# Second products of gathered expert rows moved to TensorE, with a tied order, float32 one-hots and nine row buffers

## Chip, core and metric

The kernel runs on one core of one Trainium2 chip. The metric is device time in microseconds (us) of one execution, the median of three runs. Engines: TensorE (PE, its weight loads are PEld), VectorE (DVE), ScalarE (ACT), GpSimd (POOL) and SyncE (SP); the last two issue the transfers here, GpSimd the gathers and SyncE the rest.

## What is computed

Two layers over 512 tokens of 1024 features. Each layer is a token mixer (four heads of differential attention, eight of stick-breaking attention) with a norm, and then a retrieval layer ("PEER") with a norm. The change is about the second:

```
def peer_ffn(h, w_query, sub_keys, expert_u, expert_v):
    q = (xt @ w_query).reshape(T, PEER_HEADS, 2, HALF_Q)
    scores = einsum('thpc,hpnc->thpn', q, sub_keys)
    top_s, top_i = top_k(scores, 16)              # per half of a key
    cand_s = top_s[:, :, 0, :, None] + top_s[:, :, 1, None, :]
    best_s, best_pos = top_k(cand_s, 16)          # 16 of 16384 experts per head
    gate = softmax(best_s)
    act = gelu(einsum('cd,ced->ce', xc, expert_u[ic]))      # 8 heads x 16 = 128 experts a token
    return einsum('ce,ced->cd', gc * act, expert_v[ic])
```

An expert is one row of `expert_u` and one of `expert_v`, 4 KB each. All is float32.

## The kernel before

The tokens are four blocks of 128. For blocks 0 and 1 (`BLK_A`) the experts' rows are **gathered**: for each of the 128 choices an indirect DMA on GpSimd brings one row per token, 128 rows of 4 KB (line 624, tile `row`, pool `gat` with five buffers). With rows of u, VectorE multiplies by h and sums along the row (line 634, "first products": one column of `c`); then gelu and the gate; with rows of v it adds row times coefficient to `y` (line 645, "second products"). Blocks 2 and 3 (`BLK_B`) go through products with **all** experts, called dense: 32 chunks of 512 experts. `first` (line 760) makes gelu(h . u) for both blocks, `weigh` (line 791) transposes it (line 800) and multiplies it by a dense matrix of gates, `second` (line 810) multiplies by v (lines 821 to 824). Weights and factors are split into two exact parts on ScalarE (748, 806) and VectorE (750, 807), so three products stand for one. The first seven chunks make their first products in plain float32 (line 776), before the gates are known.

`select` (line 541) finds the 16 best experts of four heads on VectorE (max, max_index, match_replace, one-hots of positions). `gates` (line 657) turns a block's choices into the dense matrix: for each token a one-hot of the expert's low digit (line 700, bfloat16, four tokens at once) and three weighted one-hots of the high digit (line 711), whose products on TensorE (line 723, three for each token) go through `st` to DRAM.

The order is the kernel's own. Pieces of work are generators ("threads") that tell before each step which engines it will hold and for how long; `run_threads` (line 110) takes the step that can start first, and gives its instructions a priority. A scheduler behind it then orders each engine's instructions by priority and its own estimate of time. Threads: `early` (the mixer of block 0), `indices` and `gathers` for blocks 0 and 1 of each layer (the four gathers take turns), and `rest` (the mixer of blocks 1, 2, 3, in which `gates` is started for blocks 2 and 3, then `dense`). The mixer's projections are lines 438 and 444, its output projection line 481, the queries line 507, the scores line 513. Buffers come from pools: `t4` (18 of 4 KB per partition), `d2` (18 of 2 KB), `st` (4), `ps` (8 in PSUM).

## Time and profile before

| | us |
|---|---|
| runs: median (lowest to highest) | 3537.8 (3537.52 to 3541.9) |
| profiled execution, span | 3535.5 |
| TensorE busy | 2765.6 (78%) |
| VectorE busy | 2937.8 (83%) |
| ScalarE busy | 1184.8 (34%) |
| GpSimd busy | 1681.0 (48%) |
| DMA moved | 1032.89 MB, mean 292 GB/s |

One execution was profiled; its span is the time from the first to the last instruction. Busy times are unions of an engine's instructions. Read the stages by what they hold: 163 to 827 us is the gathering of block 0 in layer 0, 878 to 1753 that of block 1, 1898 to 2571 and 2623 to 3508 the same in layer 1; the dense products run from 1108 to 1820 and from 2857 to 3513.

### The profile page before, as it was taken

What the parts mean: (1) busy time and instruction counts of PE and PEld (TensorE: products, weight loads), DVE (VectorE), ACT (ScalarE), POOL (GpSimd) and SP (SyncE); (2) the same over time, 40 slices, a digit from 0 to 9 for tenths busy, and PEclk for the clock granted to TensorE, in tenths of its full rate; (3) what the DMA queues carried; (4) which work ended last, traced back from release to release, by engine and by line L of the source; (5) the groups of instructions that cost most, each with busy time, mean ns of one, the idle gap of its engine ahead of it and who ended that gap; (6) DMA issues with size and microseconds to landing.
All of it is one profiled execution on the core that took longest, in us unless ns stands there. A gap on an engine that the chain in (4) does not pass through costs nothing.

```text
span 3535.5 us, 42200 instructions
## 1 busy us (share of the span) xinstructions
PE 2765.6 (78%) x14604; PEld 2214.2 (63%) x14604; DVE 2937.8 (83%) x5537; ACT 1184.8 (34%) x1900; POOL 1681.0 (48%) x1297
## 2 busy tenths in 40 slices
PE   7996474468576999999997876834694679999997
PEld 5776462366245888888776764613652468888885
DVE  2577889989998888888668678999799987888888
ACT  2114640411133444444231138404110434444442
POOL 0265645763675433334314655457536743344443
PEclk9997587579777999999998886865796689999998
DMA  5698796686769999999966987955966799999996
GB/s 228 212 329 294 246 333 201 206 302 231 261 222 360 360 347 343 349 351 348 369 222 253 331 286 237 351 177 196 337 220 232 256 367 343 349 346 354 345 344 251
DMA packets 283926, 1032.89 MB, mean 292 GB/s; under 512 B 25152, under 2 KB 91200, under 8 KB 231488
## 3 DMA queue, kind: packets, MB, share of 16 engines
q0 software_dynamic: 147456, 536.94, 42.4%
q1 hardware_dynamic: 136256, 493.26, 37.6%
q8 instruction: 115, 1.88, 0.2%
q14 instruction: 99, 0.81, 0.1%
HBM read 991.30 MB, written 38.80 MB: 291 GB/s over the span
## 4 chain that ended last, share of the span: by engine, by line
PE 40%; DVE 14%; issue 6%; DMA 5%; POOL 2%; ACT 2%; POOLq 0%; DVEq 0%; ACTq 0%
PE ps L822 7%; PE ps L821 7%; PE ps L824 6%; PE ps L786 5%; PE ps L785 5%; PE ps L784 5%; DVE row L634 3%; DMA row<-u,idx 2%; DVE ha L645 2%; POOL row L624 2%; DMA row<-v,idx 2%; PE ps L800 1%; DVE d L711 1%; DVE idf L586 1%; DVE d L579 1%
## 5 line engine op out<-in xcount | busy, mean ns | idle before, releaser
L624 POOL DMA_INDIRECT row<-v,idx x512 | 669.3, 1307 | 892.6 <-DVE ha L645 662.5
L624 POOL DMA_INDIRECT row<-u,idx x512 | 655.2, 1280 | 589.1 <-DVE row L634 375.9
L634 DVE SCALAR_TENSOR_TENSOR row<-row,ha 128x1024 f32<-128x1024 f32 x512 | 666.6, 1315 | 121.0 <-DMA row<-u,idx 118.1
L645 DVE SCALAR_TENSOR_TENSOR ha<-row,c,ha 128x1024 f32<-128x1024 f32 x508 | 700.3, 1379 | 58.0 <-DMA row<-v,idx 53.9
L750 DVE TENSOR_TENSOR t<-st,t 128x1024 fp32r<-128x1024 f32 x449 | 533.2, 1224 | 210.8 <-ACT t L748 210.7
L748 ACT ACTIVATE t<-st 128x1024 fp32r<-128x1024 f32 x456 | 453.9, 1056 | 36.6 <-PE ps L824 15.8
L723 PE MATMUL ps<-d,d 128*128 128x128 bf16 x1536 | 218.4, 295 | 207.0 <-DVE d L711 128.8
L821 PE MATMUL ps<-t,d 128*128 128x512 f32 x1024 | 314.2, 398 | 44.5 <-ACT d L806 44.5
L822 PE MATMUL ps<-t,d 128*128 128x512 f32 x1024 | 342.3, 395 | 0.0
L723 PEld LDWEIGHTS <-d 128*128 128x128 bf16 x1536 | 178.6, 121 | 234.5 <-issue 192.5
L824 PE MATMUL ps<-t,d 128*128 128x512 f32 x1024 | 316.7, 390 | 0.0
L785 PE MATMUL ps<-t,t 128*128 128x512 f32 x800 | 311.5, 389 | 0.5 <-DVE t L750 0.5
L786 PE MATMUL ps<-t,t 128*128 128x512 f32 x800 | 311.7, 390 | 0.0
L784 PE MATMUL ps<-t,t 128*128 128x512 f32 x800 | 304.2, 389 | 1.0 <-ACT t L748 1.0
L507 PE MATMUL ps<-t,st 128*128 128x128 f32 x2048 | 263.2, 293 | 35.2 <-DMA st<-w_query 35.2
L507 PEld LDWEIGHTS ps<-t,st 128*128 128x128 f32 x2048 | 257.8, 209 | 41.5 <-issue 29.5
L444 PE MATMUL ps<-t,st 128*128 128x128 f32 x2048 | 243.0, 281 | 22.2 <-ACT t L191 16.2
L444 PEld LDWEIGHTS ps<-t,st 128*128 128x128 f32 x2048 | 238.9, 197 | 28.6 <-ACT t L191 18.6
L821 PEld LDWEIGHTS ps<-t,d 128*128 128x128 f32 x1024 | 190.4, 190 | 82.4 <-ACT d L806 45.5
L822 PEld LDWEIGHTS ps<-t,d 128*128 128x128 f32 x1024 | 190.1, 190 | 47.0 <-DVE t L750 10.2
L824 PEld LDWEIGHTS ps<-t,d 128*128 128x128 f32 x1024 | 192.2, 188 | 40.9 <-DVE d L807 0.3
L806 ACT ACTIVATE d<-t 128x512 fp32r<-128x512 f32 x128 | 78.7, 632 | 410.9 <-DVE t L803 410.9
(175 smaller groups left out, 4190.8 us busy)
## 6 DMA issues: line engine op xcount, KB each, us to landing
st<-ut SPq DMA_DIRECT2D x128, 1024.0 KB
st<-vd SPq DMA_DIRECT2D x128, 1024.0 KB
st<-w_in SPq DMA_DIRECT2D x48, 1024.0 KB
st<-w_query SPq DMA_DIRECT2D x48, 1024.0 KB
gd<-st SPq DMA_DIRECT2D x32, 1024.0 KB
t<-gd SPq DMA_DIRECT2D x64, 512.0 KB
st<-w_o SPq DMA_DIRECT2D x24, 1024.0 KB
ln<-ln SPq DMA_DIRECT2D x16, 512.0 KB
```

What stands on the lines that cost most here:

```text
L444: nc.tensor.matmul(ps[:, f * P:(f + 1) * P], lhsT=w(c, slice(f * P, (f + 1) * P)), rhs=hT[:, c, :], start=(c == 0), stop=(c == DC - 1))
L507: nc.tensor.matmul(ps[:, f * P:(f + 1) * P], lhsT=w(c, slice(f * P, (f + 1) * P)), rhs=hq[b][0][:, c, :], start=(c == 0), stop=(c == DC - 1))
L624: nc.gpsimd.indirect_dma_start(out=g, out_offset=None, in_=src, in_offset=bass.IndirectOffsetOnAxis(ap=idx[s // (NSEL // 2)][:, s % (NSEL ...
L634: nc.vector.scalar_tensor_tensor(g, g, 1.0, h1, op0=ALU.mult, op1=ALU.mult, accum_out=c[:, s:s + 1])
L645: nc.vector.scalar_tensor_tensor(y, g, c[:, s:s + 1], y, op0=ALU.mult, op1=ALU.add)
L750: (nc.gpsimd if eng == "POOL" else nc.vector).tensor_tensor(lo, part, hi.bitcast(F32), op=ALU.subtract)
L784: nc.tensor.matmul(ap[b], lhsT=xhi, rhs=hi[:, c, :], start=(d == 0), stop=False)
L785: nc.tensor.matmul(ap[b], lhsT=xhi, rhs=lo[:, c, :], start=False, stop=False)
L786: nc.tensor.matmul(ap[b], lhsT=xlo, rhs=hi[:, c, :], start=False, stop=(d == DC - 1))
L821: nc.tensor.matmul(y[b][n], lhsT=shi, rhs=hi[:, n, :], start=start, stop=False)
L822: nc.tensor.matmul(y[b][n], lhsT=shi, rhs=lo[:, n, :], start=False, stop=False)
L824: nc.tensor.matmul(y[b][n], lhsT=slo, rhs=hi[:, n, :], start=False, stop=stop)
```

## The change

1. **Second products on TensorE** (`token_products`). The choices are transposed (`idxT`), so that an indirect DMA brings the 128 v rows of one token, one per partition. The coefficients are transposed too, and laid into two windows `win` of 32 x 32 columns that hold zeros but for every 32nd column. A matmul with 32 columns of a window as weights adds one token's sum to one row of a 32-row group of PSUM. A step takes two tokens and two halves of 512 columns, four matmuls in four groups of 32 rows (`quarter`), which are kept next to each other. So 64 steps replace the 128 additions of a block.
2. **Tied order** (`Traced`, `bound`). The instructions that a step emits on an engine are made to follow those of steps that were planned at least 8 us earlier on that engine, so the scheduler cannot move them far from the plan. Dots and token steps are planned six gathers behind their gather (`AWAY`), and `cost` has a resource that a step may wait for without being held up in the plan (`soft`).
3. **Gates from float32 one-hots**: two VectorE instructions for each token (one with two scalars: equal, times the gate), one float32 product instead of three in bfloat16, none on GpSimd or ScalarE.
4. **Buffers**: nine rows in flight instead of five, 12 `d2` instead of 18, 17 `t4` instead of 18.
5. `gates` gets more weight among the threads (lead 40 instead of 6), and `early` of layer 1 starts only when the gates of layer 0 are planned.

```diff
-    t4p = ctx.enter_context(tc.tile_pool(name="t4p", bufs=18))
+    t4p = ctx.enter_context(tc.tile_pool(name="t4p", bufs=17))
-    gat = ctx.enter_context(tc.tile_pool(name="gat", bufs=5))
-    d2p = ctx.enter_context(tc.tile_pool(name="d2p", bufs=18))
+    gat = ctx.enter_context(tc.tile_pool(name="gat", bufs=9))
+    d2p = ctx.enter_context(tc.tile_pool(name="d2p", bufs=12))
...
+    def bound(start):
+        for n, log in nc.log.items():
+            m = marks[n]
+            while len(m) > 1 and m[1][0] <= start - REACH:
+                m.pop(0)
+            if log and m and m[0][0] <= start - REACH:
+                for ins in log:
+                    tc.add_manual_dep(ins, m[0][1], nosync, reason="plan")
+            if log:
+                m.append((start, log[-1].name))
+                log.clear()
...
-                        spawn(gates(l, b), 6.0)
+                        spawn(gates(l, b), 40.0)
...
+    def token_products(src, idxT, c, y):
+        yield cost(lat=2.0, PE=0.3, ACT=0.4)
+        ct = psum()
+        nc.tensor.transpose(ct[:, :P], c, ident)
+        cT = a2()[:, :P]
+        nc.scalar.copy(cT, ct[:, :P])
+        H = 32
+        for s in range(2):
+            for q in range(2):
+                nc.scalar.copy(wins[q].rearrange("p (i z) -> p i z", z=H)[:, :, H - 1],
+                               cT[:, (2 * s + q) * H:(2 * s + q + 1) * H])
+            ps = psum()
+            todo = []
+            def products(i, rows):
+                at = (H - 1) * i + H - 1
+                def quarter(q, a):
+                    o = H * (2 * a + q)
+                    return nc.tensor.matmul(ps[o:o + H, :], lhsT=wins[q][:, at:at + H],
+                                            rhs=rows[q][:, a * 512:(a + 1) * 512],
+                                            start=(i == 0), stop=(i == H - 1))
+                first = quarter(1, 0)
+                with tc.high_priority(offset=90000), tc.issue_after(first.ins):
+                    for q, a in ((1, 1), (0, 0), (0, 1)):
+                        quarter(q, a)
+            for i in range(H):
+                yield cost(lat=2.1, soft="PE", PE=0.95, POOL=2.08, DMA=3.2)
+                if len(todo) == AWAY // 2:
+                    products(*todo.pop(0))
+                rows = []
+                for q in range(2):
+                    g = gat.tile([P, D], F32, name="row")
+                    t = (2 * s + q) * H + i
+                    nc.gpsimd.indirect_dma_start(out=g, out_offset=None, in_=src,
+                                                 in_offset=bass.IndirectOffsetOnAxis(ap=idxT[:, t:t + 1], axis=0))
+                    rows.append(g)
+                todo.append((i, rows))
...
+            o = a2()
+            nc.scalar.copy(o, ps)
+            for a in range(2):
+                nc.sync.dma_start(y[64 * s:64 * s + 64, a * 512:(a + 1) * 512], o[64 * a:64 * a + 64, :])
...
-            yield pace(1.14)
-            g = row(ur[l], s)
-            nc.vector.scalar_tensor_tensor(g, g, 1.0, h1, op0=ALU.mult, op1=ALU.mult, accum_out=c[:, s:s + 1])
+            yield pace(1.3)
+            if len(todo) == AWAY:
+                dot(*todo.pop(0))
+            todo.append((s, row(ur[l], s)))
...
+        if b in TOK:
+            yield from token_products(vr[l], picks[l, b][2], c, y)
...
+        def hots(t):
+            hot, w = (fold(a2(), NT) for _ in range(2))
+            for k in range(NT):
+                nc.vector.tensor_scalar(hot[:, k, :], iota_b, ijg[:, 1, t + k:t + k + 1], None, op0=ALU.is_equal)
+                nc.vector.tensor_scalar(w[:, k, :], iota_b, ijg[:, 0, t + k:t + k + 1],
+                                        ijg[:, 2, t + k:t + k + 1], op0=ALU.is_equal, op1=ALU.mult)
+            return hot, w
...
             for n in range(NT):
-                for k, w in enumerate(ws):
-                    nc.tensor.matmul(ps[:, n * P:(n + 1) * P], lhsT=hot[:, 1, :, n], rhs=w[:, :, n],
-                                     start=(k == 0), stop=(k == 2))
+                nc.tensor.matmul(ps[:, n * P:(n + 1) * P], lhsT=hot[:, n, :], rhs=w[:, n, :],
+                                 start=True, stop=True)
...
     def early(l, b):
+        if l > 0:
+            yield f"gates {l - 1} {BLK_B[-1]}"
         yield from mixer(l, [b], [(b, None)], [[b]])
```

How the order moves is seen at two places. In the built program of the change most instructions carry the line of the wrapper, L70, and are told apart by their tiles.

VectorE, gates of block 3 in layer 0, before. Lines 700 and 711 are the one-hots, line 634 the first products of block 1:

```order
1024 L700 TENSOR_TENSOR d_5240<-iota_b,d_5180 128x512 x2
1025 L634 SCALAR_TENSOR_TENSOR row,c<-row,ha 128x1024 x2
1026 L711 TENSOR_TENSOR d_5243<-d_5240,d_5181 128x512
1027 L700 TENSOR_TENSOR d_5263<-iota_b,d_5180 128x512 x2
1028 L634 SCALAR_TENSOR_TENSOR row,c<-row,ha 128x1024 x2
1029 L711 TENSOR_TENSOR d_5266<-d_5263,d_5181 128x512
```

and the end of the same gates in the change (`iota_b` marks a one-hot, `row,c<-row,ha` a first product, `ha<-ha` the residual of block 0):

```order
1243 L70 TENSOR_SCALAR d_6078<-iota_b,d_5512 128x128
1244 L70 TENSOR_SCALAR d_6079<-iota_b,d_5512 128x128
1245 L70 SCALAR_TENSOR_TENSOR ha<-ha 128x1024
1246 L70 SCALAR_TENSOR_TENSOR row,c<-row,ha 128x1024 x2
1247 L70 BN_STATS aln_st<-ha 128x6 x2
```

The first products stood between the one-hots; now they stand behind the last of them, and block 0's residual and norm with them.

TensorE, second half of dense in layer 0, before. Line 784 to 786 are first products, 822 and 824 second products:

```order
3396 L822 MATMUL ps<-t_9451,d_9207 128x512 x2
3397 L824 MATMUL ps<-t_9450,d_9208 128x512 x2
3398 L785 MATMUL ps<-t_9474,t_3051 128x512
3399 L786 MATMUL ps<-t_9473,t_3050 128x512
3400 L784 MATMUL ps<-t_9473,t_3051 128x512
```

and in the change (`row,win` is a token step, two quarters in a line):

```order
2733 L70 MATMUL ps<-t_12215,d_11981 128x512 x2
2734 L70 MATMUL ps<-t_12214,d_11982 128x512 x2
2735 L70 MATMUL ps<-row,win_115 32x512 x2
2736 L70 MATMUL ps<-row,win_114 32x512 x2
2737 L70 MATMUL ps<-t_12240,d_11971 128x512 x2
2738 L70 MATMUL ps<-t_12240,d_11981 128x512 x2
```

The token steps of block 1 stand singly among dense's matmuls, each behind its two gathers; the additions that they replace stood on VectorE among the parts of the weights.

## Rows read from the trace of the kernel before

**Rows 1.** The page: busy us of each engine, and the two large DMA queues.

```profile
PE 2765.6 (78%) x14604; PEld 2214.2 (63%) x14604; DVE 2937.8 (83%) x5537; ACT 1184.8 (34%) x1900; POOL 1681.0 (48%) x1297
...
q0 software_dynamic: 147456, 536.94, 42.4%
q1 hardware_dynamic: 136256, 493.26, 37.6%
```

**Rows 2.** Busy time by stretch: from:to, length, engines' busy us, clock, DMA share, GB/s.

```profile
147.00:440.00 293.00, 220.15 (x1432) 184.73 (x1431) 238.15 (x583) 108.86 (x215) 170.99 (x136) 0.81 0.80 279
440.00:1087.00 647.00, 397.05 (x2163) 291.63 (x2161) 608.33 (x1362) 165.17 (x321) 376.05 (x311) 0.75 0.71 252
1087.00:1820.00 733.00, 706.72 (x3334) 581.86 (x3333) 587.73 (x673) 310.00 (x399) 280.60 (x194) 0.98 0.93 346
...
2202.00:2835.00 633.00, 393.58 (x2172) 288.73 (x2171) 591.57 (x1350) 164.49 (x324) 368.32 (x301) 0.75 0.71 251
2835.00:3513.00 678.00, 653.51 (x2979) 539.20 (x2977) 563.03 (x602) 287.49 (x346) 279.47 (x186) 0.98 0.93 348
```

**Rows 3.** Groups by line on VectorE, 440 to 1087 us: busy, mean ns, idle before.

```profile
L645 DVE SCALAR_TENSOR_TENSOR ha<-row,c,ha 128x1024 f32<-128x1024 f32 x127 | 186.7, 1470 | 25.9 <-DMA row<-v,idx 24.7 <-DVE ha L645 0.2 <-issue 0.2
L634 DVE SCALAR_TENSOR_TENSOR row<-row,ha 128x1024 f32<-128x1024 f32 x73 | 106.3, 1473 | 6.0 <-DMA row<-u,idx 6.0
L700 DVE TENSOR_TENSOR d<-iota_b,d 128x512 bf16<-128x512 bf16 x122 | 67.0, 586 | 0.0
L711 DVE TENSOR_TENSOR d<-d,d 128x512 bf16<-128x512 bf16 x98 | 63.2, 673 | 0.1
```

**Rows 4.** The same view, shapes apart, whole run: a 128x128 VectorE instruction with one scalar.

```profile
L296 DVE TENSOR_SCALAR dg<-ident,rc 128x128 f32<-128x128 f32 x64 | 17.5, 293 | 0.0
```

**Rows 5.** The same view, VectorE in dense, 1110 to 1690 us (25.5 chunks).

```profile
L750 DVE TENSOR_TENSOR t<-st,t 128x1024 fp32r<-128x1024 f32 x200 | 236.3, 1220 | 90.2 <-ACT t L748 90.2
...
L634 DVE SCALAR_TENSOR_TENSOR row<-row,ha 128x1024 f32<-128x1024 f32 x52 | 64.6, 1260 | 1.4 <-DMA row<-u,idx 1.4
L807 DVE TENSOR_TENSOR d<-t,d 128x512 fp32r<-128x512 f32 x55 | 36.4, 699 | 0.4
...
L634 DVE DVE_READ_ACCUMULATOR row<-row,ha 128x1 f32 x52 | 4.2, 81 | 0.0
```

**Rows 6.** Timeline of TensorE (start us, us, instruction): two chunks' transposes that follow each other.

```profile
1383.07 1.04 PE L800 MATMUL ps<-ident,t 128*128 128x128 f32 x8
...
1405.81 1.03 PE L800 MATMUL ps<-ident,t 128*128 128x128 f32 x8
```

**Rows 7.** Timeline of TensorE: runs of equal matmuls, and the second layer's first projections.

```profile
906.58 13.04 PE L776 MATMUL ps<-st,t 128*128 128x512 f32 x30
...
1824.07 14.00 PE L481 MATMUL ps<-st,t 128*128 128x512 f32 x32 [0.81 <-ACT t L412]
...
1856.57 7.31 PE L507 MATMUL ps<-t,st 128*128 128x128 f32 x64
...
1909.45 15.75 PE L444 MATMUL ps<-t,st 128*128 128x128 f32 x119 [15.94 <-ACT t L191]
```

**Rows 8.** Timeline of TensorE: 64-column matmuls of line 373, in two column groups and in one.

```profile
1820.56 0.61 PE L824 MATMUL ps<-t,d 128*128 128x512 f32 x2
1821.10 1.58 PE L373 MATMUL ps<-d,t 128*64 128x128 f32 x16
1822.61 0.66 PE L411 MATMUL ps<-ident,t 128*128 128x128 f32 x4
...
2193.25 1.09 PE L373 MATMUL ps<-d,t 128*64 128x128 f32 x8 [0.27 <-ACT t L315]
```

**Rows 9.** Timeline of all engines: gathers on GpSimd beside line 296 on VectorE.

```profile
2188.81 0.95 POOL L624 DMA_INDIRECT row<-v,idx  x1 [1.35 <-DVE ha L645]
...
2189.33 0.47 DVE L296 TENSOR_SCALAR dg<-ident,rc 128x128 f32<-128x128 f32 x1
...
2191.07 0.95 POOL L624 DMA_INDIRECT row<-v,idx  x1 [1.31 <-DVE d L351]
```

More of the change, by code (lines that the diff above doesn't have):

```diff
@@ L47, with __init__, __getattr__, call @@
 AHEAD = 7
+TOK = [0, 1]
+REACH = 8
+AWAY = 6
 NT = 4
 NTG = len(BLK_B) * P // GT
+class Traced:
+    def __init__(self, eng, log):
+        self.eng, self.log = eng, log
+    def __getattr__(self, name):
+        f = getattr(self.eng, name)
+        if not callable(f):
+            return f
+        def call(*args, **kwargs):
+            r = f(*args, **kwargs)
+            ins = getattr(r, "ins", None)
+            if ins is not None:
+                self.log.append(ins)
+            return r
+        return call
+class TracedCore:
+    def __init__(self, nc):
+        self.log = {}
+        for n in ("tensor", "vector", "scalar", "gpsimd"):
+            self.log[n] = []
+            setattr(self, n, Traced(getattr(nc, n), self.log[n]))
+        self.sync = nc.sync
 @with_exitstack
@@ L107, in spawn @@
     def spawn(gen, lead):
-        threads.append({"gen": gen, "lead": lead, "ready": clock[0], "next": None})
+        threads.append({"gen": gen, "lead": lead, "ready": clock[0], "at": clock[0], "next": None})
+    marks = {n: [] for n in nc.log}
+    nosync = mybir.DependencyInfo(mybir.DependencyClass.NoSync, mybir.DependencyReason.DATA)
+    def bound(start):
[9 more added lines that the diff above has]
+                log.clear()
     def run_threads():
@@ L126, in run_threads @@
                     continue
-                start = max([th["ready"]] + [free[e] - slack[e] for e in th["next"][1]])
+                lat, engines, soft = th["next"]
+                start = max([th["ready"]] + [free[e] - slack[e] for e in engines if e != soft])
                 ready.append((start, th))
@@ L130, in run_threads @@
             start, th = min((x for x in ready if x[0] <= first), key=lambda x: x[1]["ready"] - x[1]["lead"])
-            lat, engines = th["next"]
+            lat, engines, soft = th["next"]
+            th["at"] = start
             for e, c in engines.items():
@@ L619, in pace @@
         def pace(dve):
-            return cost(lat=2.2, DVE=dve, POOL=1.04, DMA=1.46)
+            return cost(lat=1.2, soft="DVE" if b == BLK_A[0] else "", DVE=dve, POOL=1.04, DMA=1.6)
         def row(src, s):
@@ L638, in gathers, with add @@
         y = hap.tile([P, D], F32, name="ha")
-        for s in range(NSEL):
-            yield pace(1.2)
-            g = row(vr[l], s)
-            if s == 0:
-                nc.vector.tensor_scalar_mul(y, g, c[:, s:s + 1])
-            else:
-                nc.vector.scalar_tensor_tensor(y, g, c[:, s:s + 1], y, op0=ALU.mult, op1=ALU.add)
+        if b in TOK:
+            yield from token_products(vr[l], picks[l, b][2], c, y)
+        else:
+            def add(s, g):
+                if s == 0:
+                    nc.vector.tensor_scalar_mul(y, g, c[:, s:s + 1])
+                else:
+                    nc.vector.scalar_tensor_tensor(y, g, c[:, s:s + 1], y, op0=ALU.mult, op1=ALU.add)
+            todo = []
+            for s in range(NSEL):
+                yield pace(1.35)
+                if len(todo) == AWAY:
+                    add(*todo.pop(0))
+                todo.append((s, row(vr[l], s)))
+            for x in todo:
+                yield cost(lat=1.8, DVE=1.35)
+                add(*x)
         b2 = (l, b + 1) if b + 1 in BLK_A else (l + 1, BLK_A[0])
@@ L715, in gates, with products @@
         stg = {}
-        def products(tg, t0, hot, ws):
+        def products(tg, t0, hot, w):
             if t0 == 0:
```

79 lines of the change are left out of this document (33 added, 46 removed).

## The prediction, made before the changed kernel ran

> **What bounds the kernel now.** I read four views in this order. The page's sums show three resources that are all nearly full over the whole span: VectorE 83%, TensorE 78%, the DMA queues 42.4% + 37.6% = 80% [rows 1]. Such an average hides stages, so the table of busy time by stretch comes next [rows 2]. It shows two kinds of stretch that alternate, once per layer. From 440 to 1087 us (and 2202 to 2835) VectorE is busy 608.3 of 647 us (591.6 of 633) while TensorE is busy 397 and runs at a mean granted clock of 0.75, and DMA moves 252 GB/s: **VectorE sets the pace.** It does three jobs at once there: the second products of block 0 (line 645), the choice of experts with the one-hots of the gates, and from 880 us the first products of block 1 (line 634). From 1087 to 1820 (2835 to 3513) TensorE is busy 706.7 of 733 us at a clock of 0.98 and DMA has a share of 0.93: **TensorE sets the pace and DMA is next**, with the products of all experts ("dense"). Third, the groups of VectorE in the first kind of stretch [rows 3] give what can leave it. Fourth, the rows of single instructions give prices [rows 4 to 9].
>
> The profiled execution spans 3535.5 us; the median of the runs is 3537.8, so 2.3 us lie around the span. I make the sum on the span and add 2.3.
>
> **The change, part by part.**
>
> *Second products leave VectorE.* In 440 to 1087 the 127 additions of line 645 are 186.7 us busy, with 25.9 us of idle time before them [rows 3]; 1.47 us each. The 512 of the whole run are on no path any more in the first kind of stretch.
>
> *First products of block 1 go behind the gates.* The order shows 9 of them before the last one-hot of block 3 (none in the second layer); in the trace 73 stood there, 106.3 us and 73 reads of the accumulator at 81 ns, 5.9 us [rows 3, 5]. They are not saved: they run in the dense stretch.
>
> *One-hots in float32.* Out go lines 700 and 711 on VectorE, 67.0 + 63.2 = 130.2 us for two blocks [rows 3]. In come 256 instructions of 128x128 per block; the nearest is line 296, 17.5 us for 64, 0.273 each [rows 4], so 2 x 256 x 0.273 = 139.8. Cost 9.6 us on VectorE. GpSimd and ScalarE lose their parts of lines 700 and 711, and TensorE does 4 products for each 4 tokens instead of 12; none of them was the limit, so I price that at nothing.
>
> VectorE's work in 440 to 1087 becomes 608.3 - 186.7 - 106.3 - 5.9 + 9.6 = 319 us. How long does the stretch take then? If VectorE stayed as full as now (0.94) 319/0.94 = 339; in 147 to 440, where attention and not VectorE sets the pace, it is busy 238 of 293, 0.81 [rows 2], which gives 393. I take 0.81, since the same attention and norm waits come to light. On top comes the query projection of blocks 3 and 1, when VectorE has little to do: 512 matmuls at 7.31/64 = 0.114, 58 us, 32 of the output projection, 14 us, and about 10 us of norm and transposes: 82 us [rows 7]. The gates of block 2 now share their time with 14 token steps on TensorE (28 gathers). Beside a gather, line 296 took 0.47 us instead of 0.27, and the gather its usual 0.95 [rows 9], so 28 x 0.2 = 6 us. Together 481 instead of 647: **166 us less, in each layer.** Ends: 647 - 427 = 220 (at 0.94) and 27 (at a share of 0.60, the one of TensorE there [rows 2]).
>
> The Trainium skill, SBUF — State Buffer, section Who interferes with whom, says that a VectorE tensor_scalar in its two-port mode and GpSimd hold one port pair exclusively, and that the loser blocks fully. The rows show 0.2 us, not a gather's 0.95; by the rule the 28 gathers (18 in the second layer) would add 26 and 17 us, not 6 and 4, and the sum would be 3390.
>
> *Token steps.* A step multiplies two tokens' rows, four matmuls of 32 columns by 512 on four column groups. No such step is in the trace. A 128x512 float32 matmul takes 14.0/32 = 0.4375 us [rows 7]; four in series are 1.75, four at once 0.44. The nearest row is line 373, whose heads of odd number write the other column group: 16 of them took 1.58 us, where 8 in one group took 1.09 [rows 8], so 16 in series would take 1.09 + 8 x 0.11 = 1.97. Two groups do run at once. A visit costs something too: the second of the two of line 824 started at 1820.79, the next could have at 1821.02, and line 373 started at 1821.10; line 411 came 0.09 late likewise [rows 8]. With 0.2 for a visit and a little for the second pair's start, I take **0.68 us a step** (0.44 to 1.95). 64 steps a block are 44 us.
>
> *Dense, first layer.* A full chunk is 104 matmuls, 22.74 us [rows 6]. In the order 12 chunks hold about five token steps each, ten gathers. Their TensorE time is 22.74 + 5 x 0.68 = 26.1. Their DMA time: a gathered row set costs 0.424 x 3535.5/1024 = 1.464 us, weights 0.376 x 3535.5/493.3 = 2.695 us per MB [rows 1]; a chunk loads 4.72 MB, so 10 x 1.464 + 12.7 = 27.4 us. DMA limits there, 1.3 us a chunk. Chunks with first products hold seven rows: 10.2 + 12.7 = 23.0 us of DMA; on VectorE 8 x 1.18 + 4 x 0.66 + 7 x 1.32 = 21.3 us [rows 5], which just fits.
>
> After the gates TensorE has: 25 full chunks, 569; seven chunks with their first half done early, 22.74 x 56/104 = 12.2 each, 86; block 0 of the next layer, which before ran at the end of dense and after it and now stands at its start, 512 x 0.114 + 64 x 0.4375 + some 20 of attention, 106; 62 of the early first products, at 13.04/30 = 0.435, 27; token steps 44; DMA's excess 15; idle time as now 733 - 706.7 = 26 [rows 2, 6, 7]. Sum 873, and 30 us for the norm, the trip of h through DRAM and the transposes. So from the end of the gates to the projections of the next layer 903 us. Before it was 1087 to 1909.4, 822 [rows 7]. **Cost 80 us.** Block 0's work is paid inside dense instead of after it, and nearly all of block 1's gathers must fit in as well.
>
> *Second layer.* The first stretch again gives 166. Dense takes 678 [rows 2] and has no early block to hold: 12 chunks go from 22.74 to 27.4, +56; 13 steps at the end, +9; first products +3: **cost 68.** Tail: the result passes through a copy and a DMA, +3.
>
> *Nine row buffers.* They let a gather be issued before the buffer of five earlier is read. Where VectorE held the buffers that is a gain already counted; where DMA is full it adds nothing. The price is one t4 and six d2 buffers less; in the order a weight half still finds its place two to five halves ahead in dense, three to six before, and a half takes 2.7 us on TensorE, so nothing.
>
> Sum: -166 + 80 - 166 + 68 + 3 = -181; 3535.5 - 181 = 3354.5, and with 2.3 around it **3357 us.**
>
> **The rivals.**
>
> *Slower: the four quarters run in series.* A step then costs 1.75 + 0.2 = 1.95 us, in TensorE's own order, before every product that stands behind it. A chunk with five steps takes 22.74 + 9.75 = 32.5 instead of 27.4, 24 times: +122. The 13 steps at the end add 17, and the 64 steps in each first stretch 81, of which half lies beside idle TensorE (busy 397 of 647): +80. Total 3357 + 219 = 3576, slower than now. It decides from about 1.75 us a step on. Against it stands line 373 [rows 8]; for it, that no row has four groups.
>
> *Slower: waits take VectorE's place.* Each engine must now keep to the plan's order, so a late gather on TensorE holds the gates' products behind it, and these hold the one-hots. With VectorE at 0.60 in the first stretches they shorten by 27 us each: 3357 + 278 = 3635. It decides where each shortens by less than 76, a share of 0.66. Against it: the order has gathers six ahead of their step, and these stretches use DMA at 0.71 [rows 2].
>
> *Faster still.* VectorE stays as full as now: 220 a layer, 3357 - 108 = 3249. For it: much of that work, the choice and the gates, depends on VectorE alone.
>
> *The port lock.* If one-hots and gathers exclude each other as 28 x 0.95 and 18 x 0.95 us in the gates of block 2, the sum is 3390. The skill's sentence above is this case; the rows speak for the smaller price.
>
> *The change doesn't do what it says.* With DMA at 0.93 in dense, nine buffers may bring no more bytes there; that is the forecast already.
>
> **How the numbers follow.** Forecast 0.62, at 3357, with its own range 3280 to 3460 (steps two by two, 1.08 us, would be 3357 + 50). Faster still 0.16. Port lock 0.07. Series 0.08, waits 0.07. The range is 3225 to 3480: the two slow rivals lie above it, 0.15, and some of the fastest below. A measurement can tell about 0.2%, 7 us: faster 0.85, the same 0.02, slower 0.13.
>
> **What would show it.** In the table by stretch: the gates of block 3 end near 920 us instead of 1087, and VectorE's share in that stretch is near 0.8. The quarters of one step start within 0.1 us of each other and a step takes 0.6 to 0.8 us. In dense, chunks with first products take 23 us, those with token steps 27 to 28, with a DMA share close to 1. The projections of the second layer start near 1820 instead of 1909. The prediction is wrong if steps start one after the other, if TensorE waits for gathers in the first stretch, or if its clock falls to 1.2 GHz in dense.

## The result

| | before | change |
|---|---|---|
| median of the runs (lowest to highest), first chip | 3537.7 (3535.7 to 3541.9) | 3558.7 (3552.6 to 3565.4) |
| the same on another chip | 3543.7 (3536.4 to 3552.7) | 3536.8 (3530.6 to 3543.6) |
| profiled execution, span | 3535.5 | 3563.6 |

The ratio is 1.0061, 95% interval 1.0043 to 1.0079, on the first chip, and 0.9979 (0.9969 to 0.999) on the other, where the same program ran again. So the change is worth nothing within about half a per cent, and its sign depends on the chip. The forecast was 3357. All experiments ran beside the kernel before, whose median was 3542 to 3546 on their chips; they are compared with 3537, the change on the other chip of the table. On the three chips where the change was timed it took 3559, 3537 and 3534 us (one run); on the chips of experiments 4 and 9 and of the last two of experiment 8 it was not timed. So a difference of less than some 25 us from the change says little here.

The page of the change. Against [rows 1], VectorE lost 699 us of work and TensorE gained 264. Nearly all instructions carry the wrapper's line, L70; `row,win` is the token steps:

```profile
span 3563.6 us, 44443 instructions
...
PE 3029.1 (85%) x16148; PEld 2191.2 (61%) x16148; DVE 2238.5 (63%) x5540; ACT 1148.2 (32%) x1785; POOL 1463.9 (41%) x1170
...
q0 software_dynamic: 147456, 536.94, 41.3%
q1 hardware_dynamic: 137536, 495.36, 36.8%
...
L70 PE MATMUL ps<-row,win 128*32 128x512 f32 x2048 | 281.3, 636 | 48.6 <-DMA row<-v,idxT 48.6
```

Busy time by stretch, columns as in [rows 2]. The stretches are cut at the end of block 3's gates (907.2, 2682.5), at the end of dense in layer 0 (1906), at the next projections (1964.5) and at the end of dense in layer 1 (3549):

```profile
440.00:907.20 467.20, 385.49 (x2342) 248.52 (x2340) 335.41 (x1392) 147.68 (x268) 181.06 (x168) 0.91 0.72 264
907.20:1906.00 998.80, 918.23 (x4346) 668.01 (x4344) 568.64 (x913) 340.53 (x438) 398.88 (x280) 0.97 0.83 307
1906.00:1964.50 58.50, 4.61 (x32) 4.16 (x25) 50.55 (x80) 3.00 (x6) 44.85 (x38) 0.53 0.96 361
...
2682.50:3549.00 866.50, 803.81 (x3636) 577.98 (x3635) 508.04 (x623) 293.83 (x359) 370.34 (x269) 0.97 0.88 324
```

The stages, in us; the forecast is the prediction's own sum:

| stage | before | forecast | change | difference |
|---|---|---|---|---|
| start to the end of the gates, layer 0 | 1087 | 921 | 907 | -180 |
| to layer 1's first projections (dense) | 822 | 903 | 1057 | +235 |
| to the end of the gates, layer 1 | 926 | 760 | 718 | -208 |
| to the end (dense and tail) | 700 | 771 | 881 | +181 |

The gain in front of the gates came, and a little more of it than forecast. **Both dense stages gave all of it back.** There the miss is 154 + 110 us.

### The profile page after: what moved, and what is told of

The parts are those of the page before. It is cut to its first block, busy times and chain, and to the rows that moved or that the text cites. A ratio compares the mean times of both kernels' runs of the same rounds, so it can differ in the third digit from the quotient of the medians.

```text
span 3563.6 us, 44443 instructions
## 1 busy us (share of the span) xinstructions
PE 3029.1 (85%) x16148; PEld 2191.2 (61%) x16148; DVE 2238.5 (63%) x5540; ACT 1148.2 (32%) x1785; POOL 1463.9 (41%) x1170
## 4 chain that ended last, share of the span: by engine, by line
PE 34%; issue 12%; DVE 8%; DMA 5%; POOL 5%; ACT 3%; another core or an unknown queue 0%; POOLq 0%; SPq 0%; DVEq 0%; ACTq 0%
PE ps L70 34%; DVE d L70 4%; POOL row L70 4%; DMA t<-gd 2%; DVE t L70 1%; POOL t L70 1%; ACT d L70 1%; DVE row L70 1%; ACT L70 1%; ACT t L70 1%; DMA st<-ut 1%; DMA row<-v,idxT 1%; DVE idf L70 1%; DMA row<-u,idx 1%
## 5 line engine op out<-in xcount | busy, mean ns | idle before, releaser
L70 POOL DMA_INDIRECT row<-u,idx x512 | 672.9, 1314 | 783.2 <-DVE row L70 500.7
L70 PE MATMUL ps<-t,d 128*128 128x512 f32 (+1 forms) x3232 | 798.4, 400 | 97.6 <-ACT t L70 42.9
L70 POOL DMA_INDIRECT row<-v,idxT x512 | 540.3, 1055 | 662.5 <-PE ps L70 544.3
L70 PEld LDWEIGHTS ps<-t,d 128*128 128x128 f32 x3232 | 605.4, 194 | 286.2 <-ACT t L70 77.4
L70 DVE TENSOR_TENSOR t<-st,t 128x1024 fp32r<-128x1024 f32 x410 | 502.5, 1263 | 416.6 <-ACT t L70 348.5
L70 PE MATMUL ps<-t,t 128*128 128x512 f32 (+1 forms) x3040 | 676.5, 385 | 29.3 <-DVE t L70 15.5
L70 DVE SCALAR_TENSOR_TENSOR row<-row,ha 128x1024 f32<-128x1024 f32 x512 | 619.3, 1236 | 105.7 <-DMA row<-u,idx 99.5
L70 PEld LDWEIGHTS ps<-t,t 128*128 128x128 f32 (+1 forms) x3040 | 521.3, 199 | 168.7 <-issue 43.6
L70 PE MATMUL ps<-t,st 128*128 128x128 f32 x4096 | 488.4, 280 | 28.7 <-issue 24.7
L70 PEld LDWEIGHTS ps<-t,st 128*128 128x128 f32 x4096 | 477.9, 196 | 45.5 <-issue 40.8
L70 ACT ACTIVATE t<-st 128x1024 fp32r<-128x1024 f32 x456 | 455.5, 1051 | 119.3 <-PE ps L70 88.5
L70 PE MATMUL ps<-st,t 128*128 128x512 f32 x960 | 436.6, 610 | 38.6 <-DMA st<-ut 26.5
L70 ACT ACTIVATE t<-ps 128x512 f32<-128x512 f32 (+1 forms) x192 | 88.9, 492 | 881.7 <-PE ps L70 821.7
L70 PEld LDWEIGHTS ps<-st,t 128*128 128x128 f32 x960 | 183.1, 195 | 266.1 <-issue 240.6
L70 PE MATMUL ps<-row,win 128*32 128x512 f32 x2048 | 281.3, 636 | 48.6 <-DMA row<-v,idxT 48.6
L70 DVE TENSOR_SCALAR d<-iota_b,d 128x128 f32<-128x128 f32 x1024 | 234.1, 315 | 13.1 <-PE ps L70 7.8
L70 PE MATMUL ps<-d,d 128*128 128x128 f32 x1280 | 219.1, 305 | 21.2 <-ACT d L70 7.6
L70 PEld LDWEIGHTS ps<-d,d 128*128 128x128 f32 x1280 | 172.9, 196 | 95.6 <-issue 39.8
L70 ACT COPY t<-ps 128x512 f32<-128x512 f32 (+4 forms) x180 | 81.3, 459 | 460.0 <-PE ps L70 389.7
L70 DVE TENSOR_TENSOR t<-ps,t 128x512 f32<-128x512 f32 x128 | 83.1, 685 | 188.5 <-DMA t<-gd 139.2
L70 POOL TENSOR_TENSOR t<-d,d 128x800 f32<-128x800 bf16 x64 | 107.9, 1704 | 152.0 <-DVE d L70 141.0
L70 ACT COPY d<-ps 128x512 f32<-128x512 f32 (+3 forms) x124 | 62.8, 516 | 332.9 <-PE ps L70 323.6
```

The source lines that it names most:

```text
L70: r = f(*args, **kwargs)
```

## Experiments

**1. The same program with readable lines.** The wrapper was rewritten so that each instruction keeps its own line; nothing else moves. Line numbers from here on are the change's: 703 a token quarter, 721 and 747 the gathers of v and u, 753 a dot, 863 and 865 the high and low parts of dense's weights, 891 the plain float32 first products, 899 to 901 the split ones, 915 the transposes, 936 to 939 the second products.

> The changed kernel once more, the same instructions in the same order, but with each instruction's own line in the trace instead of the wrapper's. Every theory: 3559 us, within 0.3%. It is for reading: which matmuls fill TensorE between the end of the gates and the end of the dense products.

It took 3533.9 on another chip, 0.7% less than its first timing and outside the 0.3%. Timed again in five rounds, on a third chip:

> The changed kernel once more, timed in turn with the kernel before on this chip. Its one run beside the other experiments took 3534 us where the kernel before took 3545, and its first timing 3559 beside 3538. If the change is slower by itself: 3550 to 3560 and a ratio near 1.006; if the two sit within what differs from chip to chip: a ratio between 0.996 and 1.006.

Measured: 3536.8, the second line of the table above, so the second reading holds: the two differ by what differs from chip to chip. Groups on TensorE in this run (profiled span 3539.3, called the run with lines below), columns as in [rows 3]: first from 440 us to the end of the gates at 905, then dense of layer 0, 905 to 1965:

```profile
L703 PE MATMUL ps<-row,win 128*32 128x512 f32 x512 | 73.6, 672 | 20.7 <-DMA row<-v,idxT 20.7
L891 PE MATMUL ps<-st,t 128*128 128x512 f32 x96 | 45.2, 622 | 7.0 <-DMA st<-ut 7.0
```

```profile
L937 PE MATMUL ps<-t,d 128*128 128x512 f32 x512 | 171.8, 409 | 24.9 <-POOL t L865 17.2 <-DVE t L865 7.0
...
L900 PE MATMUL ps<-t,t 128*128 128x512 f32 x400 | 162.2, 406 | 15.5 <-DVE t L865 10.4 <-POOL t L865 5.1
...
L936 PE MATMUL ps<-t,d 128*128 128x512 f32 x512 | 153.2, 409 | 30.7 <-ACT t L863 30.7
...
L703 PE MATMUL ps<-row,win 128*32 128x512 f32 x512 | 66.3, 608 | 0.0
L891 PE MATMUL ps<-st,t 128*128 128x512 f32 x128 | 59.5, 617 | 3.4 <-DMA st<-ut 3.4
...
L253 PE MATMUL ps<-ident,ha 128*128 128x128 f32 x24 | 4.0, 324 | 58.3 <-DVE ha L270 58.3
```

The same stretches of the kernel before, 440 to 1078 and 1078 to 1909:

```profile
L776 PE MATMUL ps<-st,t 128*128 128x512 f32 x224 | 104.0, 623 | 0.0
```

```profile
L822 PE MATMUL ps<-t,d 128*128 128x512 f32 x512 | 171.0, 395 | 0.0
L824 PE MATMUL ps<-t,d 128*128 128x512 f32 x512 | 158.3, 390 | 0.0
L821 PE MATMUL ps<-t,d 128*128 128x512 f32 x512 | 156.6, 397 | 20.0 <-ACT d L806 20.0
L785 PE MATMUL ps<-t,t 128*128 128x512 f32 x400 | 155.9, 390 | 0.5 <-DVE t L750 0.5
```

Three things are to be seen. The plain first products all stood in front of the gates before (224 records); now 96 do and 128 stand in dense, 59.5 us. The token steps stand half in front and half in dense, 66.3 us there. And the waits for the split parts grew from 20.5 to 71.1 us: TensorE now stands still ahead of lines 936, 937 and 900, 22.3 us of it for low parts that GpSimd makes. Line 253 is the first work of the next layer, behind dense; it waits 58.3 us for block 1's norm.

**2. Which block's token steps pay.**

```diff
-TOK = [0, 1]
+TOK = [0]      # in the next: TOK = []
```

> One number changed: only block 0's second products go to TensorE, those of block 1 are additions on VectorE again. Theory T (TensorE sets the pace of dense, and its token steps at 281.3/256 = 1.10 us lengthen it): 64 steps a layer less, 2 x 70 us, and 128 additions of about 1.26 us fit on VectorE, busy only 569 of 999 and 508 of 867 us there: 3559 - 141 = 3418. Rival D (dense is held by DMA, with nine gathers in flight): the same bytes move, 3545 to 3565. Rival V (VectorE's additions are late again and hold the row buffers): 3500 to 3540.

Measured: 3478.9, ratio 0.982 (0.980 to 0.984).

> No second products on TensorE at all; tied order, float32 one-hots and nine row buffers stay. Theory T: block 0's 128 additions come back between the one-hots, 187 us on VectorE, so the gates of block 3 end some 60 to 90 us later in each layer than in the change, while dense loses all 64 steps: 3418 + 60 to 180, between 3480 and 3600, with the end of block 3's gates near 980 instead of 907. If the tied order and the buffers, not the products, are what costs the time in dense, it stays above 3600.

Measured: 3662.0, ratio 1.033 (1.031 to 1.035); block 3's gates ended at 1013 instead of 900. So block 0's steps are worth 183 us and block 1's cost 58 (3478.9 against 3536.8). Without any, the rest of the change is 117 us slower than the kernel before, although its gates of layer 0 end 74 us earlier (1013 against 1087): behind them it loses some 190 us, no less than the change does with its steps (175 to 208, by chip). So that loss does not need the token products. Which other part of the change brings it was not separated: the tied order and the plan's price of a gather are tried in experiments 5 and 8, the float32 one-hots, the nine buffers and the gates' weight by no run. Block 1's steps cost less than the 141 expected, since in layer 1 the additions now end last. Dense of layer 1 in the run with block 0 alone (columns as in [rows 2]):

```profile
2608.00:3340.00 732.00, 687.70 (x2935) 533.11 (x2936) 552.90 (x657) 276.46 (x335) 299.13 (x201) 0.98 0.90 332
3340.00:3474.00 134.00, 41.44 (x189) 33.49 (x187) 118.58 (x111) 15.03 (x18) 68.10 (x61) 0.67 0.77 284
```

In its last 134 us TensorE is busy 41 and VectorE 119: dense is done, block 1's additions are not.

**3. The price of a step.** 128 columns for each quarter:

```diff
-return nc.tensor.matmul(ps[o:o + H, :], ..., rhs=rows[q][:, a * 512:(a + 1) * 512],
+return nc.tensor.matmul(ps[o:o + H, :P], ..., rhs=rows[q][:, a * 512:a * 512 + P],
```

> Token steps with 128 columns instead of 512 for each quarter; three quarters of the second products of blocks 0 and 1 are left out (the sums of the first 128 columns of each half are written four times). Same gathers, same waits, same number of matmuls; a quarter takes 2 x 0.114 instead of 2 x 0.4375 us, so 256 x 0.65 = 166 us less on TensorE, half of it in dense. Theory T: 83 to 110 us less, 3450 to 3476. Rival D (DMA): 3540 to 3560. If DMA is close behind TensorE in the chunks with token steps, about 45 us less, 3515.

Measured: 3496.9, ratio 0.986 (0.982 to 0.990), 40 us less than the change, between the theories; its runs spread from 3478 to 3509. Timeline of TensorE (columns as in [rows 6]), the transposes at the start of two chunks with five token steps each, in the change (layer 0) and in this run (layer 1; the change's chunks there take 28.33 us too):

```profile
1593.86 0.60 PE L915 MATMUL ps<-ident,t 128*128 128x128 f32 x4
...
1622.19 0.60 PE L915 MATMUL ps<-ident,t 128*128 128x128 f32 x4
```

```profile
3194.26 0.60 PE L915 MATMUL ps<-ident,t 128*128 128x128 f32 x4
...
3220.22 0.38 PE L915 MATMUL ps<-ident,t 128*128 128x128 f32 x2
```

28.33 us become 25.96: 0.47 us a step, of the 0.65 that TensorE saves. In these chunks TensorE does set the pace, and the 27.4 us that the prediction gave DMA as the limit is no limit. Over 12 such chunks a layer that makes 57 us for both layers, of which 40 arrive.

**4. The plain first products.** A quarter of them:

```diff
-for c in range(4):
+for c in range(1):
```

> The change with three quarters of the first seven chunks' plain float32 first products left out (two of eight slices of the features are multiplied). Loads, gathers and waits stay. In the trace these products take TensorE 44 us before the end of the gates of block 3 and 57 us behind it, in each layer; before the change all 102 us lay in front of it. Theory N (what spilled behind the gates is paid in full, since TensorE sets the pace there): 2 x 43 us less in dense and up to 2 x 20 in front of the gates, where TensorE is busy 385 of 457 us: 3537 - 90 = 3447, between 3410 and 3460. If they lie beside other waits (for weights, the gates' trip through DRAM): 3515 to 3540.

Measured: 3501.6, ratio 0.987 (0.985 to 0.989), 35 us less. Theory N holds for two fifths only. TensorE in dense of layer 1, this run:

```profile
L936 PE MATMUL ps<-t,d 128*128 128x512 f32 x512 | 157.3, 406 | 31.0 <-ACT d L921 20.9 <-ACT t L863 10.1
...
L891 PE MATMUL ps<-st,t 128*128 128x512 f32 x32 | 21.4, 803 | 16.4 <-DMA st<-ut 16.4
```

The products fell from 59 to 21.4 us, but TensorE then waits 16.4 us for their weights and 31.0 in front of line 936 (10.4 and 15.8 in the change). So what spilled lies partly beside waits that come out once it is gone.

**5. The tied order.**

```diff
-REACH = 8
+REACH = 1000000
```

> One number changed: the distance over which the order is tied is raised without bound, so the scheduler may move instructions freely as before; everything else of the change stays. Rival O (the tied order puts gathers behind GpSimd's waiting pow instructions and a chunk's weight splits behind ScalarE's gelu, 1.15 us a chunk with first products): 3480 to 3515. If the ties cost nothing, the time stays within 0.5% of the change, 3530 to 3565.

Measured: 3539.6, ratio 0.9986 (0.9973 to 0.9999). Chunks with dots (first products of block 1) took 23.2 us instead of 23.97, but the whole is the same: the ties cost nothing, and the rival falls.

**6. The seams of the gathers.** The change gathers no v row while the last dots run, and none for a block's second half before the first half's steps are done. In this experiment three pairs of v rows are gathered between the last six dots, and the 64 steps form one row:

```diff
-for s in range(2):
-    ...
-    for i in range(H):
+for j in range(len(todo), 2 * H):
+    ...
+    todo.append((j, pair(src, idxT, j)))
```

> Gathers run on across the two seams of a block: the first three token steps' v rows are gathered while the last dots are made, and the second half's rows while the first half's steps end. Nothing else is changed. In the trace of the change no gather is issued for 71 to 78 us (layer's block 0) and 44 to 45 us (block 1) between u and v, and 26 to 32 us between the halves. Theory B (these seams idle DMA in a kernel that wants it elsewhere, and TensorE waits about 20 us a seam in dense): 40 to 100 us less than the change. If TensorE alone holds the time (theory T) only its idle time at the seams of dense goes, 10 to 40 us.

Measured: 3506.5, ratio 0.9895 (0.988 to 0.991), 30 us less: what theory T expects, not theory B.

> The same, with token steps for block 0 alone and block 1's second products as additions on VectorE. With the seams, block 0 alone took 3479 us; there dense ended some 80 us before the run did, and the last gathers and additions of block 1 held the end. Theory B: the gathers end earlier, 3380 to 3430. If VectorE's additions and not the late gathers hold that end: 3460 to 3480.

Measured: 3457.6, ratio 0.975 (0.973 to 0.978): 21 us less than with the seams, not the 50 or more of theory B, and just below the other range.

**7. Block 0 of layer 1 later in dense.** In the change's trace VectorE makes no dot between 914.01 and 971.14, and TensorE stands still for 54.58 us behind dense. The wait of `early` was moved from the gates to chunk 24:

```diff
-yield f"gates {l - 1} {BLK_B[-1]}"
+yield f"chunk {l - 1} 24"
```

> The change with one thing moved: block 0 of layer 1 goes through its mixer late in dense of layer 0 (when chunk 24 of 32 is planned) instead of right behind the gates. In the change VectorE stands 58 us (909 to 968) at that block's first attention instruction and 38 us (1112 to 1150) at its choice of experts, with block 1's dots and so all gathers queued behind; and after dense TensorE is busy only some 5 us of the 58 before the next projections. Theory W (these waits are part of what was given back in dense of layer 0): 40 to 90 us less than the change, 3447 to 3497 on this chip, and 970 to 1020 us instead of 1063 from the end of the gates to the next projections. If the block's 106 us of TensorE cost the same wherever they stand: 0 to 15 us less.

Measured: 3576.6, ratio 1.010 (1.007 to 1.012), 40 us **more**. Dense of layer 0 took 1060 us as before; the next gates came 35 us later, as block 0's gathers did (the last v row at 2595 instead of 2563).

> The late block 0 together with gathers that run on across the seams and token steps for block 0 alone (3458 us without the late block). Theory W: 40 to 90 us less, 3368 to 3418. If it costs the same anywhere: 3440 to 3460.

Measured: 3504.3, again 47 us more than without. Theory W falls: that block costs dense the same wherever it stands, and early is better.

**8. The plan's price of a gather.**

```diff
-POOL=1.04, DMA=1.6)
+POOL=1.04, DMA=1.2)      # and 2.4 instead of 3.2 for a pair
```

The kernel before had 1.46 us here; that the change raised it to 1.6 is one more of its parts.

> Gathers that run on across the seams, token steps for block 0 alone (3458 us), and in the plan a gather is priced at 1.2 us of DMA instead of 1.6, so that 7 instead of 6 or 7 dots and additions of block 1 stand in each dense chunk. Theory G (the four turns of gathers, one behind the other, are a second bound beside TensorE, and the plan, not the hardware, spaces them): 15 to 50 us less, 3408 to 3443. If DMA is full there, the chunks lengthen as much: 3450 to 3465.

Measured: 3532.1, ratio 0.997. Dense of layer 1 was 26 us shorter (794 instead of 820), but the gates ended 57 us later in layer 0 and 104 in layer 1, counted from the start (977 and 2742). Further down, with the lower price for block 1 alone, the gates keep their place; so it is block 0's gathers and steps, spaced closer, that took it.

> Both: the late block 0 and the lower price of a gather in the plan, with token steps for block 0 alone and no seams. If theories W and G both hold: 3330 to 3400, the fastest so far. If neither: about 3455.

Measured: 3504.9, 50 us above what neither theory would give. ("No seams" means that the gathers run on across them.) With the lower price for block 1 alone:

> Gathers across the seams and token steps for block 0 alone (3458 us); the plan's price of a gather is lowered from 1.6 to 1.2 us for block 1 only. With the lower price for both blocks dense took 986 and 794 us instead of 982 and 820, but the gates of block 3 ended 57 and 49 us later. If both belong to the block whose price was changed: the gates as early as in that kernel (920 and 2638 us on its own time scale) and dense 26 us shorter in the second layer: 3415 to 3440. If the place of the gates depends on block 1's price too: 3460 to 3530.

Measured: **3418.9, ratio 0.963 (0.961 to 0.965)**, faster than both kernels; gates at 918 and 2629, dense of layer 1 789 us. That is 39 us less than at the plan's old price for block 1.

> The same with four instead of seven chunks whose first products are plain float32; three more chunks a layer go through exact halves (10.9 us of TensorE instead of 14). Theory N: about 15 us a layer less where these products had spilled behind the gates, 3390 to 3425. If ScalarE's and VectorE's splits of three more chunks hold the dense products back: no gain, 3420 to 3460.

Measured: 3415.2, ratio 0.963 (0.961 to 0.965): no gain that can be told.

**9. Are gathers the second limit?**

```diff
 for s in range(NSEL):
+    if b == BLK_A[1] and s % 2:
+        continue
```

> The change with every second u gather and first product (dot) of block 1 left out, 64 of its 256 gathers in each layer; half of block 1's coefficients are zero. TensorE's work is the same. Theory T (TensorE holds dense by itself): only the 1.15 us that chunks with dots took beyond 22.74 go, for some nine chunks a layer, 3515 to 3537. Theory G (the gathers, one turn behind the other, are as close a limit): 64 x 1.46 us of DMA less in each layer, 3350 to 3430.

Measured: 3490.3, ratio 0.985 (0.982 to 0.988), 47 us less, between the two theories. The gain is all in dense of layer 1, 825 us instead of 878; layer 0 gained nothing from 64 gathers less (1764 us from its gates to the next, 1756 in the change). Layer 1 in two parts, cut where the gathers end:

```profile
2664.00:3230.00 566.00, 542.00 (x2550) 383.27 (x2550) 290.96 (x337) 197.78 (x243) 258.06 (x188) 0.98 0.91 343
3230.00:3489.00 259.00, 231.03 (x1040) 183.72 (x1038) 85.52 (x69) 93.87 (x115) 183.89 (x76) 0.97 0.50 175
```

TensorE is busy 773 of 825 us, with no gather left in the last 259; in the change it is 805 of 878. Of the 53 us that dense of layer 1 gains, 24 are not what was asked about: 80 records of plain first products stood behind the gates (35.0 us) instead of 128 (59.0). And a second thing moved: the low parts that GpSimd makes (experiment 10), whole run, in the run with lines and in this one:

```profile
L865 POOL TENSOR_TENSOR t<-st,t 128x1024 fp32r<-128x1024 f32 x46 | 118.2, 2591 | 126.1 <-ACT t L863 102.6 <-issue 12.9 <-PE ps L937 8.0
```

```profile
L869 POOL TENSOR_TENSOR t<-st,t 128x1024 fp32r<-128x1024 f32 x139 | 350.3, 2545 | 199.7 <-ACT t L867 122.2 <-PE ps L919 57.5 <-PE ps L941 7.8
```

With fewer gathers in the plan, GpSimd got three times as many low parts, so this run mixes fewer gathers with what experiment 10 finds to be costly.

> The same with token steps of 128 instead of 512 columns (three quarters of the second products of blocks 0 and 1 left out too). With all gathers the narrow steps gave 40 us of the 83 to 110 expected. Theory G: with the gathers out of the way they give their full price, 80 to 110 us less than the other run of this pair. Theory T: 40 us less, as before.

Measured: 3445.7, 45 us less than the other, nearly the 40 that narrow steps gave with all gathers. That is theory T's answer, but this run too has 139 low parts on GpSimd, so whether the gathers are a second limit stays open.

**10. Who splits the weights.** The seam of block 1 in layer 0, timeline of GpSimd in the change:

```profile
1478.76 0.93 POOL L721 DMA_INDIRECT row<-v,idxT  x1 [0.30 <-issue]
1503.11 20.82 POOL L865 TENSOR_TENSOR t<-st,t 128x1024 fp32r<-128x1024 f32 x8 [23.42 <-ACT t L863]
1524.08 0.96 POOL L721 DMA_INDIRECT row<-v,idxT  x1
```

GpSimd waits 23.42 us for ScalarE's high part, then makes eight low parts, 2.6 us each, and all gathers stand behind. TensorE's line 937 waits 5.87 us for one of them at 1537.40. The plan chooses between VectorE and GpSimd by which it believes is free first: 7 of the 456 low parts were on GpSimd before (the row below), 46 are in the change (512 in the expectation is a miscount), at the start of dense in layer 0 and at each seam of the gathers:

```profile
L750 POOL TENSOR_TENSOR t<-st,t 128x1024 fp32r<-128x1024 f32 x7 | 18.9, 2705 | 13.7 <-PE ps L304 9.3 <-ACT t L748 4.3
```

```diff
-eng = pick(POOL=2.8, DVE=1.2)
+eng = pick(DVE=1.2)
```

> The change with the low parts of the dense weights all made on VectorE (1.26 us each) instead of 46 of 512 on GpSimd (2.59 us each, with gathers queued behind). TensorE waits 17.2 us in dense of layer 0 and 7.9 us in dense of layer 1 right before matmuls for a part from GpSimd. If that is a cause of dense's idle time: 20 to 40 us less than the change (0.987 to 0.993 of the kernel before). If the wait only shows there and another comes last without it: within 10 us of the change, a ratio of 0.995 to 1.001.

Measured: **3465.3, ratio 0.978 (0.976 to 0.980)**, 71 us less, where 20 to 40 were expected. Dense took 1015 and 853 us instead of 1060 and 878. TensorE in dense of layer 0, this run:

```profile
L937 PE MATMUL ps<-t,d 128*128 128x512 f32 x512 | 169.6, 406 | 12.5 <-DVE t L865 11.6
L900 PE MATMUL ps<-t,t 128*128 128x512 f32 x400 | 160.6, 402 | 7.9 <-DVE t L865 7.8
L936 PE MATMUL ps<-t,d 128*128 128x512 f32 x512 | 153.1, 411 | 26.1 <-ACT t L863 26.0
...
L253 PE MATMUL ps<-ident,ha 128*128 128x128 f32 x24 | 4.9, 375 | 33.9 <-DVE ha L270 33.9
```

Dense of layer 0 by its busy times (columns as in [rows 2]), in the run with lines and in this one:

```profile
905.00:1965.00 1060.00, 924.16 (x4365) 672.98 (x4364) 618.65 (x990) 343.16 (x443) 446.13 (x318) 0.94 0.83 310
```

```profile
901.00:1916.00 1015.00, 921.20 (x4369) 673.41 (x4370) 599.40 (x992) 343.54 (x444) 360.76 (x275) 0.95 0.85 316
```

TensorE's busy time is the same; its idle time fell from 136 to 94 us. The waits ahead of the first three lines fell from 71.1 to 46.5 us, the one behind dense (line 253) from 58.3 to 33.9. The gathers, which had gaps of 44 and 27 us between 1150 and 2100 us, have none over 21 there. The edit takes away all 46 parts, the seven of the kernel before too, and the plan orders the rest anew; it was not tried together with experiment 8.

The count of these parts moved in other experiments as well, since each changes the plan: 28 with block 0 alone, 25 with no token steps, 31 without the seams, 22 and 25 in the two fastest runs. A part of what those runs gained or lost may be this.

## Why the prediction was wrong, step by step

The forecast was 3357, and 3537 to 3559 were measured. The gain in front of the gates came; the sum for dense failed, above all in the idle time of TensorE.

**VectorE's work in front of the gates: the number right, the reason in part.** Forecast 166 us a layer, measured 180 and 208. VectorE was busy 335 us where 319 were counted. But the sum divided by a share of 0.81 for VectorE, and the share is 0.72 (319 of 481 us, as the sum ends, is 0.66). What took over is TensorE, busy 385 of 467 us (0.83) where it had been 397 of 647: its granted clock rose from 0.75 to 0.91 as it grew busier, which the sum did not contain. So that the length came out is partly luck, and the 42 us more in layer 1 are not explained.

**The step's price: right mechanism, wrong size.** The four quarters run at once, and that rival is out. Timeline of TensorE in the change, one step among dense products, and three at the end of dense:

```profile
1602.31 1.06 PE L703 MATMUL ps<-row,win 128*32 128x512 f32 x8
1603.31 1.20 PE L936 MATMUL ps<-t,d 128*128 128x512 f32 x4
...
1903.34 2.78 PE L703 MATMUL ps<-row,win 128*32 128x512 f32 x24
1960.70 1.94 PE L253 MATMUL ps<-ident,ha 128*128 128x128 f32 x8 [54.58 <-DVE ha L270]
```

A step is four matmuls and **eight records**. A float32 matmul of the program is two records here: the 32 of line 481 in [rows 7], 14.00 us, are 16 matmuls, at 0.875 us. So a step is 2 x 0.4375 plus a visit, 281.3 / 256 = 1.10 us, not 0.68. (For the projections the sum counted records, so their 58 us stand; for the steps and the plain first products it counted the program's matmuls and paid one record for each.) In the sum it hardly shows: the forecast had 44 us of steps and 15 of excess DMA for layer 0, 59, and the row says 66.3; for layer 1 it had 56 + 9 = 65, and 68.8 us are there. The chunk of 28.33 us is 22.74 + 5 x 1.1, TensorE's, where 27.4 was forecast as DMA's. Two errors met; that the chunk's forecast is near is luck.

**Plain first products behind the gates: a term that was mis-sized.** Layer 0: the sum has 62 matmuls at the price of one record, 27 us; 128 records, which are 64 matmuls, took 59.5. The count was right and the price was half. Layer 1: the sum has at most its 3 us for "first products"; the same 128 records took 59.0. Experiment 4 took three quarters of them away and got 35 us back, so of this error less than the whole arrives in the time. Why they moved is argued, not shown: the shorter stretch left TensorE 82 us idle instead of 250, and these products had lived in that idle time. It can't be all of it, for in the run without token steps TensorE was idle 226 of 573 us there (440 to 1013 us), and 80 of 224 records still stood behind the gates. The gates' greater weight in the plan may have pushed them back; no run tried it alone.

**Idle time of TensorE in dense: the step that failed.** The sum put it at "idle time as now", 26 us, read from the kernel before, and 30 us for the norm between the layers, for which it gives no row. Measured in layer 0: 1060 - 924 = 136 in the run with lines. By its rows 71.1 are waits for the split parts and 58.3 the wait for block 1's norm. The first was charged to nobody: the buffers' part of the prediction counted tiles, not who splits. Experiment 10 shows one cause: the plan put 46 low parts on GpSimd instead of 7, in front of gathers, where it believed VectorE busy. Without them TensorE's idle time in layer 0 is 94 us, and the run 71 us shorter. What causes those 94 (46.5 ahead of the three lines, 33.9 behind dense) is not shown. For the wait behind dense in the run with lines two rows tell a part: GpSimd's step of block 1's norm is done at 1932, and VectorE goes on with it at 1955, behind 17 dots of the next layer's block 0 that stand ahead of it in VectorE's order:

```profile
1931.17 0.89 POOL L266 TENSOR_TENSOR aln_rs<-aln_ve,mhalf 128x1 f32<-128x1 f32 x1
```

```profile
1955.23 0.81 DVE L268 TENSOR_SCALAR ha<-ha,aln_mv,aln_rs 128x1024 f32<-128x1024 f32 x1
```

The rest of the miss in layer 0 is busy time, 924 us where the sum has 832: 32 of these 92 are the plain products, 22 the steps (15 of them were in the sum as DMA's excess), and the others are not settled.

**Chunks with dots** take 23.97 us (line 915 at 1325.99 and 1349.96 in the run with lines), forecast 23.0. At 13 to 17 chunks a layer that is some 15 us each; experiment 5 gave most of it back in these chunks and nothing in all.

**The rivals.** Series: out. Waits in VectorE's place: not in front of the gates, where it was put, and not by the tied order (experiment 5); but waits are what happened in dense, on GpSimd instead of TensorE. The port lock: out. In the run with lines the one-hots of line 827 that run beside a gather took 0.35 us on the mean, the others 0.33, and none more than 0.55; a lock for a gather's 0.95 would show. **Nine buffers** brought no more bytes a second in dense (DMA share 0.83 and 0.88, against 0.93), as said.

Of the 264 us missed in dense, experiment 10 brings back 71 (all 46 low parts, seven of which are not new) and experiment 4 brings back 35 with three quarters of the plain products. The norm's wait is 28 us above its 30, but part of it went in experiment 10 too, so these are not to be added up. The rest is spread over waits that change places when one is taken away: experiments 3, 4 and 9 each gave back a quarter to two fifths of the time that their edit takes off TensorE or DMA. It is not settled further.

## What to carry to other kernels

Idle time of one engine in a stretch that another engine bounds is where other work lives: before shortening the stretch, list that work and look where it will go. Here 128 of 224 records went into the next stretch, and TensorE's idle time in dense, taken over from the old kernel, more than doubled. When a plan chooses engines by its own estimate of who is free, look after every change at what moved to the slow engine, above all if that engine also issues the transfers; one such choice cost 71 us here. And count such choices again in every experiment, since each edit makes the plan anew. Calibrate a matmul's price by counting program instructions against trace records in the same row.

## What was not expected of the hardware

A 128x512 float32 matmul leaves two records of 0.4375 us each. Four column groups of 32 run fully at once: eight records in 1.06 us, three steps in 2.78 us, so 0.86 for each further step. The low part of a weight (128x1024) takes 1.26 us on VectorE and 2.59 on GpSimd. In dense of layer 0 of the change the median u gather held GpSimd 1.68 us, the median v gather 0.94. It is not the row alone: in the kernel before, whose v rows VectorE adds, the median v gather in dense took 1.55. What makes the difference was not tried.
